# A two-layer decoder on one core: one weight pool for all stages, two loads on another queue, block transposes further apart, operand addresses at one residue

## The chip, the cores and the metric

The kernel runs on one core of a Trainium2 chip. The time is device microseconds of one execution. Of the kernel before, three runs are shown: 2102.8, 2106.49 and 2108.27 us, median 2106.49.

A core has five engines that run side by side, each with its own instruction stream: TensorE (PE) multiplies matrices and also turns (transposes) tiles, VectorE (DVE) and ScalarE (ACT) work on elements, GpSimd (POOL) does a few small things here, and SyncE (SP) only issues loads and stores (DMA). PE reads its operands from SBUF, the core's working memory, and writes to PSUM, a small memory of eight banks that DVE and ACT read. Engines wait for each other through semaphores.

## The reference

256 tokens of width 2048 pass through two layers; all values are float32. Each layer computes, with RMS norms in front:

- attention of its own kind plus attention to 256 memory tokens. Layer a has native sparse attention: a projection `h @ a_w_in`, compressed keys by a small two-layer network, a block-selected and a windowed branch, gated and added. Layer b reads one shared key/value pair (`rms_norm(h) @ w_kv_shared`) with three dilated windows merged by their softmax denominators.
- an output projection (`@ w_out`) added to h,
- a SwiGLU feed-forward with 5632 hidden columns, added to h:

```
h + (silu(y @ w_gate) * (y @ w_up)) @ w_down,   y = rms_norm(h)
```

A last RMS norm gives the output (256, 2048). The feed-forwards hold most of the arithmetic: three matrices of 2048 x 5632 for each layer.

## The kernel before

**How products are made.** Matmuls take float32 operands in a reduced form, so each operand is split into a high part and a rest: `split` (L75) lets ACT write the rounded high part (L77, or L80 with a gain) and DVE the remainder (L78 or L81). `mm3` (L84) then issues three matmuls: high by high (L86), rest of the activations by high weights (L87), high by rest of the weights (L88). A weight chunk is loaded by `load_w` (L93) into a tile `raw` (128 x 1024) on SP's queue, and split into `whi` and `wlo`. A chunk feeds twelve matmuls of 512 columns: four PSUM banks by three.

**The stages.** There are four, each opened by `open_phase` (L56): attention of layer a, feed-forward of layer a ("fa"), attention of layer b, feed-forward of layer b ("fb"). A stage opens its own weight pool (four `raw`, and three `whi`/`wlo` in attention or two in the feed-forward), its own PSUM pools and further tiles; `phase.close()` frees them. The pools of the next stage take the same memory, and the first instruction that uses such a pool waits until the old one is free. In the feed-forward stages seven PSUM banks hold products and one, `aux`, is for turns; in attention `aux` has three or four.

**Feed-forward.** The 11 blocks of 512 hidden columns are worked in three portions, of 4, 4 and 3 blocks (`PORTIONS`). `Group` (L840) is the work of one block (gate and up) or of one half of a portion's down projection (`Lazy`, L1016). Part of it is done by a seven-product scheme in place of eight: `Group.steps` (L876) has seven steps, each with one product of a quarter weight tile of 1536 columns (`q11` and so on, split into `qhi` and `qlo`; nine matmuls), with sums of weight quarters made by DVE (L885, L892, L900, L912). The rest of a block are plain chunks (`plain`, L920). `run_groups` (L936) lays the seven steps of the next group between the plain chunks of the present one; `spacing` (L931) says how many plain chunks stand before each step.

**Turning a block.** When a block's banks are finished, `gate_up` (L974) makes the hidden values as two tiles `hb` (one for each half of the tokens; ACT L982, DVE L983). They have to be turned before the down projection can use them: `Paired.heads` (L297) gives two steps, each with four transposes by PE into an `aux` bank (L305) and then the evacuation by ACT and DVE. For the columns that take part in the seven-product scheme the values first go to a tile `xf`, DVE makes four sums of it (L277 to L280) and both are split (L281). The residual is turned in the same way after the output projections (`residual_block`, L322; transposes L227 or L290).

**Order.** PE's order is the written one. Side steps are put among the matmuls by ticks: a `Side` (L117) counts one tick for every `mm3`, and a step runs when its tick is reached. What `deferred` collects is taken by the next group or product. For the turns of a block the ticks are 5 and 8 (L985), for the residual 3 and 5 (L327). The order on the other engines and on the queues is fixed when the kernel is built, by a planner that plays the program through with a cost for each instruction (`manual_schedule(engines={PE})`, L1304, leaves it all engines but PE).

**Around the change of stage from "fa" to attention b** (L1045 to L1080): the table `cs` and the mask `mask_b` are loaded on SP's queue, the stored memory keys `mb` on GpSimd's; `scaled_tables` (L346) multiplies the table by the token norms before `rope` uses it at the end of the first product.

Of the kernel before, what the change touches and what calls it, by code (L numbers as in the profile page):

```python
# [41 lines left out]
def decoder_trunk(ctx: ExitStack, tc: tile.TileContext, a: dict, out: bass.AP):  # L42
    nc = tc.nc

    const = ctx.enter_context(tc.tile_pool(name="const", bufs=1))
    dram = ctx.enter_context(tc.tile_pool(name="dram", bufs=1, space=bass.MemoryType.DRAM))
    xp = ctx.enter_context(tc.tile_pool(name="xp", bufs=1))
    small = ctx.enter_context(tc.tile_pool(name="small", bufs=6))
    work = ctx.enter_context(tc.tile_pool(name="work", bufs=1))
    work.tile([P, 96], F32, name="padw")  # L50
    phase = ctx.enter_context(ExitStack())
    aux_stack = ExitStack()
    fbufs = [1]
    fpool = wp = wbufs = mm_ps = aux_ps = mm_tags = None

    def open_phase(name, raws, parts, mms, auxs):  # L56
        nonlocal wp, wbufs, mm_ps, mm_tags, aux_ps
        wp = phase.enter_context(tc.tile_pool(name="w" + name, bufs=1))
        wbufs = raws, parts
        mm_ps = phase.enter_context(tc.tile_pool(name="m" + name, bufs=1, space=PSUM))  # L60
        mm_tags = mms
        phase.enter_context(aux_stack)
        aux_ps = aux_stack.enter_context(tc.tile_pool(name="x" + name, bufs=auxs, space=PSUM))
# [29 lines left out]
    def load_w(src, ncols, gain=None, after=None):  # L93
        ck = src.shape[1] // ncols
        raw = wp.tile([P, 1024], F32, tag="raw", name="raw", bufs=wbufs[0])
        rv = raw[:, :ck * ncols]
        if after is None:
            nc.sync.dma_start(rv, src)
        else:
            for q in range(ck):  # L100
                nc.sync.dma_start(rv[:, q * ncols:(q + 1) * ncols], src[:, q * ncols:(q + 1) * ncols])
                after(q)
        rv = rv.rearrange("p (c n) -> p c n", n=ncols)
        hl = []
        for tag in ("whi", "wlo"):
            t = wp.tile([P, 1024], F32R, tag=tag, name=tag, bufs=wbufs[1])
            hl.append(t[:, :ck * ncols].rearrange("p (c n) -> p c n", n=ncols))
        if gain is None:
            split(hl[0], hl[1], rv)
        else:  # L110
            for c in range(ck):
                split(hl[0][:, c, :], hl[1][:, c, :], rv[:, c, :], gain(c))
        return [(hl[0][:, c, :], hl[1][:, c, :]) for c in range(ck)]
# [73 lines left out]
    const.tile([P, 32], F32, name="padc")  # L187
    open_phase("a", 4, 3, ATT, 3)
    ac = phase.enter_context(tc.tile_pool(name="ac", bufs=1))
# [5 lines left out]
    w2 = ac.tile([P, 2, 2, HD], F32, name="w2")  # L195
    ac.tile([P, 8], F32, name="pada")

# [53 lines left out]
    class Paired:  # L251
# [18 lines left out]
        def new_f(self):  # L270
            return fpool.tile([P, NSL, P], F32, tag="xf", name="xf", bufs=fbufs[0])

        def finish(self, q, f):
            n = 4
            if self.sums:
                n = NSL
                nc.vector.tensor_sub(f[:, 4, :], f[:, 0, :], f[:, 3, :])  # L277
                nc.vector.tensor_sub(f[:, 6, :], f[:, 1, :], f[:, 0, :])
                nc.vector.tensor_sub(f[:, 5, :], f[:, 4, :], f[:, 1, :])
                nc.vector.tensor_add(f[:, 7, :], f[:, 2, :], f[:, 5, :])  # L280
            split(self.S[0][:, q, :n, :], self.S[1][:, q, :n, :], f[:, :n, :])  # L281

# [38 lines left out]

    def residual_block(ps, nb, ssq, op):  # L322
        for tt in range(2):
            hb = h[:, tt, nb * 512:(nb + 1) * 512]
            nc.vector.tensor_add(hb, ps[tt], hb)
            square_sum(ssq[:, tt, nb:nb + 1], hb)
        deferred.extend(at([lambda k2=k2: op.turn(nb, k2) for k2 in range(2)], 3, 5))  # L327

# [272 lines left out]
    def compress(kv, toks):  # L601
# [30 lines left out]
        def turn():  # L632
            e = st["e"]
            tr = aux_tile()
            for i in range(2):
                nc.tensor.transpose(tr[:, i * 60:(i + 1) * 60], e[:, i * P:(i + 1) * P], ident[:60, :60])
            z = work.tile([P, 2, 60], F32, tag="cz", name="cz", bufs=1)
            nc.scalar.activation(z.rearrange("p i m -> p (i m)"), tr[:, :120], AF.Copy)
            s = work.tile([P, 2, 30], F32, tag="cs", name="csg", bufs=1)
            zs = z[:, :, 0:30]  # L640
# [172 lines left out]
    def project_out(name, nk, ready, gi):  # L813
        op = Paired(new_x(), KT, lambda k: gains[:, gi, k:k + 1])
        ssq = new_ssq()
        ob = wblocks(name, 4, nk // CK)
        n = nk // CK
        side = take()
        g = [Gemm(ob[i], osx, 512, nk) for i in range(2)]
        side.rate = max(1, 8 / (2 * ready))  # L820
        for i in range(2):
            g[i].run(0, ready, side)
        side.flush()
        for i in range(2):
            side = take()
            g[i].run(ready, n, side)
            side.flush()
            residual_block(g[i].ps, i, ssq, op)
        for nb in range(2, 4):
            ps = gemm(ob[nb], osx, 512, nk)  # L830
            residual_block(ps, nb, ssq, op)
        return op, finish_rstd(ssq, 4)
# [7 lines left out]
    class Group:  # L840

        def __init__(self, op, quarters, rest, done, rest_done=None):
# [84 lines left out]

    def spacing(n):  # L931

        base = {16: (3, 2, 2, 2, 2, 2, 2), 10: (2, 1, 1, 2, 1, 2, 1), 6: (1, 1, 1, 1, 0, 1, 1)}[n]
        return base, n - sum(base)

    def run_groups(groups):  # L936
        for i, g in enumerate(groups):
# [4 lines left out]
            if nxt is not None and nxt.q is not None:  # L942
                base, left = spacing(n)
                for p, s in enumerate(nxt.steps(side)):
# [15 lines left out]
    def ffn(pre, op, f_r, last):  # L960
        gq, gs = a[pre + "_gu_q"], a[pre + "_gu_s"]
        groups = []
        for pi, (b0, b1) in enumerate(PORTIONS):
# [9 lines left out]

            def gate_up(g, j, hop=hop):  # L974
                up = g.bank[3]
# [4 lines left out]
                for tt in range(2):  # L980
# [3 lines left out]
                    hb.append(t)  # L984
                deferred.extend(at(hop().heads(j, hb), 5, 8))  # L985

# [11 lines left out]
            for n2 in range(2):  # L998
# [13 lines left out]

                groups.append(Lazy(hop, [dq[pi, n2, i] for i in range(4)], [ds[n2, c] for c in range(nk - 2 * NPR)], done, rest_done))
        run_groups(groups)

    class Lazy(Group):  # L1016
        def __init__(self, hop, *args):
            super().__init__(None, *args)
            self.hop = hop

# [6 lines left out]
    def open_ffn(name):  # L1027
        nonlocal fh, fq, fpool
        fbufs[0] = 2
        open_phase(name, 4, 2, FFN, 1)  # L1030
        fh = phase.enter_context(tc.tile_pool(name="h" + name, bufs=1))
# [7 lines left out]
    def to_b(ps, nb):  # L1039
        nonlocal xb  # L1040
        if xb is None:
            xb = Plain()
        residual_block(ps, nb, ssq_b, xb)

# [4 lines left out]

    open_phase("b", 4, 3, ATT, 4)  # L1050
    ac = phase.enter_context(tc.tile_pool(name="acb", bufs=1))
    cs = ac.tile([P, 2, 2, HD], F32, name="cs")
    nc.sync.dma_start(cs, a["cs"])
    pc = stack.enter_context(tc.tile_pool(name="pc", bufs=1))
    att = (pc, 4, 6)
    mask_b = pc.tile([P, 2, 3, T], BF16, name="mask_b")
    nc.sync.dma_start(mask_b, a["mask_b"])
    mb = [pc.tile([P, 1024], F32R, name=f"mb{i}") for i in range(4)]
# [259 lines left out]
```

## Time and profile before

| what | value |
|---|---|
| profiled execution | 2106.48 us, span 2104.7 us |
| PE busy | 2033.8 us (97%), 9417 matmuls |
| weight load of PE | 1680.9 us (80%) |
| DVE busy | 1644.3 us (78%) |
| ACT busy | 1190.3 us (57%) |
| loads and stores | 400.74 MB, mean 190 GB/s |
| mean granted TensorE clock | 0.991 |

Time is read so: busy shares say which engine could set the end; the waits say who waited for whom. In lines of the timeline, the first number is the start in us from the begin of the span, the second the duration, then engine, line of the kernel, operation, output and inputs, shapes; in brackets stands how long the engine was idle before it and what ended that. In lines of stretches, after the width come the busy us of PE, weight load, DVE, ACT and GpSimd with their instruction counts, the granted clock, the share of DMA time and GB/s. SPq and POOLq are DMA issues on those queues.

### The profile page before, as it was taken

Reading aid. Unit: us, or ns where it says so; the run is one execution under the profiler, and the core shown is the slowest. Engines: PE = TensorE matmul, PEld = TensorE weight load, DVE = VectorE, ACT = ScalarE, POOL = GpSimd, SP = SyncE. Lnnn points to the kernel's source line nnn. Section 1 sums busy time; section 2 is a strip of 40 time slices with the busy share of each in tenths; the row PEclk is TensorE's granted clock in tenths of the full one; section 3 lists DMA queues with packets and bytes.
Section 4 is the critical chain, followed back from the end, with each engine's and each line's share of the span. In section 5 each row is a group of like instructions: output and inputs, shape, how many; then the busy total and the mean of one; then the engine's idle time right before and its main releaser. Section 6 shows DMA issues by size and latency. Waiting matters only on the chain.

```text
span 2104.7 us, 25507 instructions
## 1 busy us (share of the span) xinstructions
PE 2033.8 (97%) x9417; PEld 1680.9 (80%) x9417; DVE 1644.3 (78%) x2097; ACT 1190.3 (57%) x1552; POOL 9.6 (0%) x30
## 2 busy tenths in 40 slices
PE   9999999999999999999988999989999999999998
PEld 7888888778778887788876788868778887788886
DVE  6677897578888888787876678768888888888755
ACT  7656666556555565555654555656555555555544
POOL 0000000000000000000000000000000000000000
PEclk9999999999999999999999999999999999999999
DMA  8857634476555665556542754366655665556454
GB/s 311 274 184 244 206 102 146 140 251 203 180 180 194 217 199 180 174 203 223 190 169 80 233 171 150 111 252 198 199 175 185 204 216 188 181 186 216 149 193 158
DMA packets 104669, 400.74 MB, mean 190 GB/s; under 512 B 12128, under 2 KB 12512, under 8 KB 104160
## 3 DMA queue, kind: packets, MB, share of 16 engines
q1 hardware_dynamic: 103680, 395.97, 56.5%
q0 software_dynamic: 576, 2.10, 0.3%
q8 instruction: 74, 1.21, 0.2%
q10 hardware_dynamic: 288, 1.05, 0.1%
q14 instruction: 51, 0.42, 0.1%
HBM read 394.87 MB, written 4.19 MB: 190 GB/s over the span
## 4 chain that ended last, share of the span: by engine, by line
PE 84%; DVE 9%; issue 3%; DMA 2%; ACT 2%; SPq 0%; DVEq 0%; POOLq 0%; POOL 0%; ACTq 0%
PE mm L86 26%; PE mm L87 26%; PE mm L88 26%; DVE wlo L78 3%; DVE qlo L78 2%; DVE q L885 1%; PE aux L227 1%; ACT qhi L77 1%; PE aux L305 1%; PE aux L88 1%; PE aux L87 1%; PE aux L86 1%; ACT whi L77 1%; DVE hTlo L78 1%; DVE hb L983 1%
## 5 line engine op out<-in xcount | busy, mean ns | idle before, releaser
L77 ACT ACTIVATE whi<-raw 128x1024 fp32r<-128x1024 f32 (+1 forms) x476 | 498.0, 1047 | 522.0 <-PE mm L87 451.2
L78 DVE TENSOR_TENSOR wlo<-raw,whi 128x1024 fp32r<-128x1024 f32 (+1 forms) x476 | 573.4, 1206 | 214.5 <-ACT whi L77 212.8
L86 PE MATMUL mm<-whi,xhi 128*128 128x512 f32 (+1 forms) x1376 | 540.1, 393 | 19.1 <-ACT whi L77 9.8
L88 PE MATMUL mm<-wlo,xhi 128*128 128x512 f32 (+1 forms) x1376 | 533.8, 388 | 0.8 <-DVE wlo L78 0.7
L87 PE MATMUL mm<-whi,xlo 128*128 128x512 f32 (+1 forms) x1376 | 533.0, 387 | 0.0
L78 DVE TENSOR_TENSOR qlo<-q,qhi 128x1536 fp32r<-128x1536 f32 x210 | 368.5, 1757 | 97.2 <-ACT qhi L77 95.5
L77 ACT ACTIVATE qhi<-q 128x1536 fp32r<-128x1536 f32 x210 | 311.8, 1485 | 135.5 <-PE mm L87 128.2
L86 PEld LDWEIGHTS mm<-whi,xhi 128*128 128x128 f32 x1376 | 260.7, 189 | 68.3 <-ACT whi L77 10.6
L88 PEld LDWEIGHTS mm<-wlo,xhi 128*128 128x128 f32 x1376 | 260.3, 189 | 57.0 <-DVE wlo L78 3.5
L87 PEld LDWEIGHTS mm<-whi,xlo 128*128 128x128 f32 x1376 | 260.8, 190 | 48.2
L86 PE MATMUL mm<-whi,hThi 128*128 128x512 f32 x464 | 181.3, 391 | 0.0
L88 PE MATMUL mm<-wlo,hThi 128*128 128x512 f32 x464 | 180.8, 390 | 0.4 <-DVE wlo L78 0.4
L87 PE MATMUL mm<-whi,hTlo 128*128 128x512 f32 x464 | 180.6, 389 | 0.0
L88 PE MATMUL mm<-qlo,xhi 128*128 128x512 f32 x420 | 163.9, 390 | 1.2 <-DVE qlo L78 1.2
L86 PE MATMUL mm<-qhi,xhi 128*128 128x512 f32 x420 | 164.3, 391 | 0.0
L87 PE MATMUL mm<-qhi,xlo 128*128 128x512 f32 x420 | 163.5, 389 | 0.0
L81 DVE SCALAR_TENSOR_TENSOR wlo<-raw,gains,whi 128x512 fp32r<-128x512 f32 x160 | 113.8, 748 | 50.6 <-ACT whi L80 50.3
L80 ACT ACTIVATE whi<-raw,gains 128x512 fp32r<-128x512 f32 x160 | 107.6, 716 | 64.6 <-PE mm L87 49.4
L86 PE MATMUL mm<-whi,ohi 128*128 128x512 f32 x256 | 101.7, 397 | 1.7 <-ACT whi L80 1.7
L88 PEld LDWEIGHTS mm<-wlo,hThi 128*128 128x128 f32 x464 | 87.1, 188 | 19.0 <-DVE wlo L78 0.8
L87 PEld LDWEIGHTS mm<-whi,hTlo 128*128 128x128 f32 x464 | 87.2, 188 | 17.8
L86 PEld LDWEIGHTS mm<-whi,hThi 128*128 128x128 f32 x464 | 87.1, 188 | 17.7
(273 smaller groups left out, 2471.5 us busy)
## 6 DMA issues: line engine op xcount, KB each, us to landing
raw<-in_a_gu_s_dram SPq DMA_DIRECT2D x100, 512.0 KB, 4.0
raw<-in_b_gu_s_dram SPq DMA_DIRECT2D x100, 512.0 KB, 3.7
q<-in_a_gu_q_dram SPq DMA_DIRECT2D x40, 768.0 KB, 5.5
q<-in_b_gu_q_dram SPq DMA_DIRECT2D x40, 768.0 KB, 5.5
raw<-in_a_dn_s_dram SPq DMA_DIRECT2D x52, 512.0 KB, 3.6
raw<-in_b_dn_s_dram SPq DMA_DIRECT2D x40, 512.0 KB, 3.9
q<-in_a_dn_q_dram SPq DMA_DIRECT2D x24, 768.0 KB, 5.5
raw<-in_a_w_out_dram SPq DMA_DIRECT2D x32, 512.0 KB, 3.5
```

Of the source, the lines that this page charges most:

```text
L77: nc.scalar.activation(hi, src, AF.Copy)
L78: nc.vector.tensor_sub(lo, src, hi.bitcast(F32))
L80: nc.scalar.activation(hi, src, AF.Copy, scale=gain)
L81: nc.vector.scalar_tensor_tensor(lo, src, gain, hi.bitcast(F32), op0=ALU.mult, op1=ALU.subtract)
L86: nc.tensor.matmul(o, l[0], r[0], start=start, stop=False, skip_group_check=more)
L87: nc.tensor.matmul(o, l[1], r[0], start=False, stop=False, skip_group_check=more)
L88: nc.tensor.matmul(o, l[0], r[1], start=False, stop=stop, skip_group_check=more)
L227: nc.tensor.transpose(ps[:, i * P:(i + 1) * P], s, ident)
L305: nc.tensor.transpose(ps[:, i * P:(i + 1) * P], tok[tt][:, i * P:(i + 1) * P], ident)
L885: nc.vector.tensor_add(self.q11, self.q11, self.q12)
L983: nc.vector.scalar_tensor_tensor(t, (g.bank[2], up)[tt], f_r[:, tt:tt + 1], t, op0=ALU.mult, op1=ALU.mult)
```

## The change

- `wp`, the weight pool, is opened once for the whole kernel, in front of the others: four `raw` and three `whi`/`wlo` in every stage. `open_phase` no longer makes one.
- `cs` and `mask_b` of the second layer are issued from GpSimd's queue.
- The turns of a block go from ticks 5 and 8 to 6 and 14; for the second block of a three-block portion to 4 and 10. The turns of the residual get ticks of their own: 4 and 10 after the last output projection block, and (4, 9), (14, 19), (3, 5), (7, 9) after the last down projection of layer a.
- In the last block of a three-block portion, the next group's steps are laid out by another list: five plain chunks before the first step, none before the second, one before each other.
- `finish` splits the four turned slots first and makes the sums in a tile of their own (`xs`), split after that, so one split of eight slots becomes two of four; `xf` is half as large.
- Padding tiles change in size, and `cz` and `csg` move to another pool, so that tiles start at other addresses.

```diff
     const = ctx.enter_context(tc.tile_pool(name="const", bufs=1))
+    wp = ctx.enter_context(tc.tile_pool(name="wp", bufs=4))
...
-    work.tile([P, 96], F32, name="padw")
+    work.tile([P, 20], F32, name="padw")
...
-    def open_phase(name, raws, parts, mms, auxs):
-        nonlocal wp, wbufs, mm_ps, mm_tags, aux_ps
-        wp = phase.enter_context(tc.tile_pool(name="w" + name, bufs=1))
-        wbufs = raws, parts
+    def open_phase(name, mms, auxs):
+        nonlocal mm_ps, mm_tags, aux_ps
...
-        raw = wp.tile([P, 1024], F32, tag="raw", name="raw", bufs=wbufs[0])
+        raw = wp.tile([P, 1024], F32, tag="raw", name="raw")
...
-            t = wp.tile([P, 1024], F32R, tag=tag, name=tag, bufs=wbufs[1])
+            t = wp.tile([P, 1024], F32R, tag=tag, name=tag, bufs=3)
...
-    ac.tile([P, 8], F32, name="pada")
+    ac.tile([P, 16], F32, name="pada")
...
         def finish(self, q, f):
-            n = 4
+            split(self.S[0][:, q, :4, :], self.S[1][:, q, :4, :], f)
             if self.sums:
-                n = NSL
-                nc.vector.tensor_sub(f[:, 4, :], f[:, 0, :], f[:, 3, :])
...
-            split(self.S[0][:, q, :n, :], self.S[1][:, q, :n, :], f[:, :n, :])
+                s = fpool.tile([P, 4, P], F32, tag="xs", name="xs", bufs=1)
+                nc.vector.tensor_sub(s[:, 0, :], f[:, 0, :], f[:, 3, :])
...
+                split(self.S[0][:, q, 4:, :], self.S[1][:, q, 4:, :], s)
...
-    def residual_block(ps, nb, ssq, op):
+    def residual_block(ps, nb, ssq, op, ticks=(3, 5)):
...
-        deferred.extend(at([lambda k2=k2: op.turn(nb, k2) for k2 in range(2)], 3, 5))
+        deferred.extend(at([lambda k2=k2: op.turn(nb, k2) for k2 in range(2)], *ticks))
...
-            residual_block(ps, nb, ssq, op)
+            residual_block(ps, nb, ssq, op, (3, 5) if nb == 2 else (4, 10))
...
-    def spacing(n):
+    def spacing(n, late):
 
         base = {16: (3, 2, 2, 2, 2, 2, 2), 10: (2, 1, 1, 2, 1, 2, 1), 6: (1, 1, 1, 1, 0, 1, 1)}[n]
+        if late:
+            base = (5, 0, 1, 1, 1, 1, 1)
...
-                deferred.extend(at(hop().heads(j, hb), 5, 8))
+                deferred.extend(at(hop().heads(j, hb), *((4, 10) if late and j == 1 else (6, 14))))
...
-                groups.append(Lazy(hop, [dq[pi, n2, i] for i in range(4)], [ds[n2, c] for c in range(nk - 2 * NPR)], done, rest_done))
+                groups.append(Lazy(n2 == 0 and b1 - b0 < 4, hop, [dq[pi, n2, i] for i in range(4)], [ds[n2, c] for c in range(nk - 2 * NPR)], done, rest_done))
...
-        residual_block(ps, nb, ssq_b, xb)
+        residual_block(ps, nb, ssq_b, xb, ((4, 9), (14, 19), (3, 5), (7, 9))[nb])
...
-    nc.sync.dma_start(cs, a["cs"])
+    nc.gpsimd.dma_start(cs, a["cs"])
...
-    nc.sync.dma_start(mask_b, a["mask_b"])
+    nc.gpsimd.dma_start(mask_b, a["mask_b"])
```

More of the change, by code (lines that the diff above doesn't have):

```diff
@@ L53, in decoder_trunk @@
     fbufs = [1]
-    fpool = wp = wbufs = mm_ps = aux_ps = mm_tags = None
-    def open_phase(name, raws, parts, mms, auxs):
-        nonlocal wp, wbufs, mm_ps, mm_tags, aux_ps
-        wp = phase.enter_context(tc.tile_pool(name="w" + name, bufs=1))
-        wbufs = raws, parts
+    fpool = mm_ps = aux_ps = mm_tags = None
+    def open_phase(name, mms, auxs):
+        nonlocal mm_ps, mm_tags, aux_ps
         mm_ps = phase.enter_context(tc.tile_pool(name="m" + name, bufs=1, space=PSUM))
@@ L187, in decoder_trunk @@
     const.tile([P, 32], F32, name="padc")
-    open_phase("a", 4, 3, ATT, 3)
+    open_phase("a", ATT, 3)
     ac = phase.enter_context(tc.tile_pool(name="ac", bufs=1))
@@ L270, in new_f @@
         def new_f(self):
-            return fpool.tile([P, NSL, P], F32, tag="xf", name="xf", bufs=fbufs[0])
+            return fpool.tile([P, 4, P], F32, tag="xf", name="xf", bufs=fbufs[0])
         def finish(self, q, f):
-            n = 4
+            split(self.S[0][:, q, :4, :], self.S[1][:, q, :4, :], f)
             if self.sums:
-                n = NSL
-                nc.vector.tensor_sub(f[:, 4, :], f[:, 0, :], f[:, 3, :])
-                nc.vector.tensor_sub(f[:, 6, :], f[:, 1, :], f[:, 0, :])
-                nc.vector.tensor_sub(f[:, 5, :], f[:, 4, :], f[:, 1, :])
-                nc.vector.tensor_add(f[:, 7, :], f[:, 2, :], f[:, 5, :])
-            split(self.S[0][:, q, :n, :], self.S[1][:, q, :n, :], f[:, :n, :])
+                s = fpool.tile([P, 4, P], F32, tag="xs", name="xs", bufs=1)
+                nc.vector.tensor_sub(s[:, 0, :], f[:, 0, :], f[:, 3, :])
+                nc.vector.tensor_sub(s[:, 2, :], f[:, 1, :], f[:, 0, :])
+                nc.vector.tensor_sub(s[:, 1, :], s[:, 0, :], f[:, 1, :])
+                nc.vector.tensor_add(s[:, 3, :], f[:, 2, :], s[:, 1, :])
+                split(self.S[0][:, q, 4:, :], self.S[1][:, q, 4:, :], s)
         def turn(self, nb, k2):
@@ L636, in turn @@
                 nc.tensor.transpose(tr[:, i * 60:(i + 1) * 60], e[:, i * P:(i + 1) * P], ident[:60, :60])
-            z = work.tile([P, 2, 60], F32, tag="cz", name="cz", bufs=1)
+            z = ac.tile([P, 2, 60], F32, tag="cz", name="cz", bufs=1)
             nc.scalar.activation(z.rearrange("p i m -> p (i m)"), tr[:, :120], AF.Copy)
-            s = work.tile([P, 2, 30], F32, tag="cs", name="csg", bufs=1)
+            s = ac.tile([P, 2, 30], F32, tag="cs", name="csg", bufs=1)
             zs = z[:, :, 0:30]
@@ L840, in decoder_trunk @@
     class Group:
+        late = False
         def __init__(self, op, quarters, rest, done, rest_done=None):
@@ L942, in run_groups @@
             if nxt is not None and nxt.q is not None:
-                base, left = spacing(n)
+                base, left = spacing(n, nxt.late)
                 for p, s in enumerate(nxt.steps(side)):
@@ L972, in hop, with gate_up @@
                 return hp["op"]
-            def gate_up(g, j, hop=hop):
+            def gate_up(g, j, hop=hop, late=b1 - b0 < 4):
                 up = g.bank[3]
@@ L1011, in done, with __init__ @@
                                 nc.vector.tensor_add(hbk, ps[tt], hbk)
-                groups.append(Lazy(hop, [dq[pi, n2, i] for i in range(4)], [ds[n2, c] for c in range(nk - 2 * NPR)], done, rest_done))
+                groups.append(Lazy(n2 == 0 and b1 - b0 < 4, hop, [dq[pi, n2, i] for i in range(4)], [ds[n2, c] for c in range(nk - 2 * NPR)], done, rest_done))
         run_groups(groups)
     class Lazy(Group):
-        def __init__(self, hop, *args):
+        def __init__(self, late, hop, *args):
             super().__init__(None, *args)
-            self.hop = hop
+            self.late, self.hop = late, hop
         def steps(self, side):
@@ L1029, in open_ffn @@
         fbufs[0] = 2
-        open_phase(name, 4, 2, FFN, 1)
+        open_phase(name, FFN, 1)
         fh = phase.enter_context(tc.tile_pool(name="h" + name, bufs=1))
@@ L1048, in decoder_trunk @@
     phase.close()
-    open_phase("b", 4, 3, ATT, 4)
+    open_phase("b", ATT, 4)
     ac = phase.enter_context(tc.tile_pool(name="acb", bufs=1))
     cs = ac.tile([P, 2, 2, HD], F32, name="cs")
-    nc.sync.dma_start(cs, a["cs"])
+    nc.gpsimd.dma_start(cs, a["cs"])
     pc = stack.enter_context(tc.tile_pool(name="pc", bufs=1))
```

## The prediction

> **What bounds the kernel now.** I read the page first, for the busiest engine, then the waits of that engine, then the stretches of granted clock, and last the timeline at each place where the waits sit.
>
> ```profile
> span 2104.7 us, 25507 instructions
> PE 2033.8 (97%) x9417; PEld 1680.9 (80%) x9417; DVE 1644.3 (78%) x2097; ACT 1190.3 (57%) x1552; POOL 9.6 (0%) x30
> ```
>
> PE sets the end. The change takes no matmul away, so it can only win what PE loses: the time it waits, and the time it runs at a lowered clock. The waits of PE (total us, times, longest):
>
> ```profile
> PE aux L305 <- DVE hTlo L78: 23.6, 14, 1.8
> PE mm L86 <- ACT whi L80: 11.0, 3, 9.3
> PE mm L86 <- ACT whi L77: 9.8, 2, 4.9
> PE aux L227 <- DVE xlo L81: 5.4, 2, 2.8
> PE aux L227 <- DVE xlo L78: 2.8, 2, 1.4
> PE mm L86 <- ACT hThi L77: 1.5, 1, 1.5
> PE mm L87 <- DVE hTlo L78: 1.2, 1, 1.2
> ```
>
> L305 are the turns of a finished feed-forward block (four 128x128 transposes each), L227 the turns of the residual, and the long waits of L86 are the three changes of stage. Stretches of the trace, with the granted clock before the last two numbers:
>
> ```profile
> 420.00:434.00 14.00, 10.87 (x32) 8.11 (x33) 8.37 (x9) 5.64 (x8) 0.00 (x0) 0.65 0.78 297
> 526.00:570.00 44.00, 42.48 (x192) 34.91 (x191) 37.06 (x35) 25.59 (x28) 0.00 (x0) 1.00 0.57 186
> 1061.00:1065.00 4.00, 4.00 (x12) 3.13 (x11) 1.76 (x1) 1.97 (x2) 0.00 (x0) 0.57 0.00 0
> 1161.00:1168.00 7.00, 6.54 (x21) 5.34 (x22) 4.25 (x7) 4.54 (x8) 0.00 (x0) 0.56 1.05 394
> 1374.00:1379.00 5.00, 4.09 (x9) 2.79 (x10) 2.45 (x2) 1.88 (x2) 0.00 (x0) 0.52 1.03 404
> ```
>
> After each long wait the clock falls to about half for some microseconds. Width times missing clock gives 14 x 0.35 + 4 x 0.43 + 7 x 0.44 + 5 x 0.48 = 12.1 us; about 1.1 of it fell while PE was still waiting, which leaves 11.0. The ordinary block (526 to 570) keeps its clock in spite of its 1.5 to 1.8 us wait.
>
> **The change part by part.** *One weight pool.* Today each stage has its own pool, and the first load of a stage waits until the old pool is free:
>
> ```profile
> 414.80 0.39 PE L86 MATMUL mm<-whi,ohi 128*128 128x512 f32 x1
> 415.03 0.39 PE L87 MATMUL mm<-whi,olo 128*128 128x512 f32 x1
> 415.25 0.39 PE L88 MATMUL mm<-wlo,ohi 128*128 128x512 f32 x1
> 415.67 1.28 SPq L98 DMA_DIRECT2D raw<-in_a_gu_dram  x3
> 415.68 0.69 DVE L325 TENSOR_TENSOR h<-mm,h 128x512 f32<-128x512 f32 x1 [0.67 <-PE mm L88]
> 420.53 0.79 PE L86 MATMUL mm<-whi,xhi 128*128 128x512 f32 x1 [4.89 <-ACT whi L77]
> ```
>
> The load leaves at 415.67, right after the last matmul of the attention stage (415.25 + 0.39). Landing, rounding and weight loading take the rest of the 4.89 us. With one pool the buffers rotate through the boundary, so up to four raw tiles and two or three rounded ones are ready before the stage ends. What ends last then is the PSUM pool, which still belongs to the stage: the first new matmul has to wait for the residual add at 415.68 (0.69 us), so some 0.8 us of wait stay. The end of the second layer's attention has the same form. The third boundary:
>
> ```profile
> 1150.17 2.73 DVE L325 TENSOR_TENSOR h<-mm,h 128x512 f32<-128x512 f32 x4 [1.31 <-PE mm L88]
> 1152.20 0.33 SPq L1053 DMA_DIRECT2D cs<-in_cs_dram  x1
> 1153.19 23.52 SPq L98 DMA_DIRECT2D raw<-in_w_kv_shared_dram  x10
> 1152.72 1.24 POOL L1060 DMA_DIRECT2D mb<-memkv  x2 [734.36 <-DVE h L325]
> cs<-in_cs_dram SPq DMA_DIRECT2D x1, 256.0 KB, 2.7
> mb<-memkv POOLq DMA_DIRECT2D x4, 512.0 KB, 9.8
> ```
>
> Table and mask stand on SP's queue ahead of the weights, and their tiles lie where the feed-forward tiles were. On one queue they would hold back every prefetch behind them; on GpSimd's they don't. The last add ends at 1152.90, so here too about 0.8 us stay of 9.3. Waits of the three boundaries: 9.3 + 9.8 = 19.1 today, 3 x 0.8 = 2.4 afterwards. The waits that remain are shorter than the 1.8 us of a block turn, after which the clock stays, so the 11.0 us of low clock go too; the piece at 1061 hangs on the next part.
>
> What the move to GpSimd may cost: the scaled tables (four DVE instructions) wait for the cs load, and the weight roundings behind them in DVE's order wait with them. The load may take anything from the 2.7 us of its own row on SP to the 9.8 us of the neighbouring rows on GpSimd's queue. At 2.7 nothing is lost. At 9.8 the tables are done some 12 us after the last matmul, while three rounded chunks of 12 matmuls each (0.227 us apart, by the starts 414.80 to 415.25) and the turns between them keep PE busy for about 11 from its restart: a loss of 2 us or less. I take 0, since the 9.8 us rows ran against ten weight loads, of which four will already be in.
>
> The Trainium skill speaks against this move: "SBUF — State Buffer", box on the "DVE blocks DMA" trap, says that a load from GpSimd's queue needs GpSimd to write its descriptors, and that some DVE instructions lock it out meanwhile. The 9.8 us against 2.7 agree with it. By that rule the sum would be at most the 2 us worse that I keep as a bound.
>
> *Three rounded weight buffers in the feed-forward stages instead of two.* No instruction more; ACT and DVE may run one chunk (12 x 0.227 = 2.7 us) further ahead. DVE is busy 37.06 of 44 us in a block, and 37 of 42 once the wait is gone, so it has the room. I count no gain for it alone.
>
> *Turns further apart.* The feed-forward stages have one PSUM bank for turns, so the second turn waits for the evacuation of the first:
>
> ```profile
> 532.90 0.60 PE L305 MATMUL aux<-ident,hb 128*128 128x128 f32 x4
> 533.82 1.22 DVE L78 TENSOR_TENSOR wlo<-raw,whi 128x1024 fp32r<-128x1024 f32 x1
> 534.96 1.75 DVE L78 TENSOR_TENSOR qlo<-q,qhi 128x1536 fp32r<-128x1536 f32 x1
> 536.63 0.42 DVE L78 TENSOR_TENSOR hTlo<-aux,hThi 128x256 fp32r<-128x256 f32 x1
> ```
>
> The evacuation stands on DVE behind a weight rounding and a quarter rounding and ends at 537.05, 4.15 us after the turn began. The two turns are 3 ticks apart, a tick being three matmuls or 0.68 us: 2.0 us. They go to 6 and 14, 8 ticks or 5.4 us, 1.3 more than the bank needs. So the 23.6 us go. The residual's turns go from two pairs at ticks 3 and 5 to 4, 9, 14, 19 (5 ticks, 3.4 us) and 4, 10 (4.1 us): their evacuation took at most about 3.4, so 5.4 + 2.8 go as well. Splitting pairs costs four more changes between the two kinds of matmul, some 0.1 us each: 0.4.
>
> A later turn can miss its reader. Most blocks are read 30 ticks later. The exception is the last block of the three-block portion, whose tokens the first down product reads directly:
>
> ```profile
> 1103.94 0.68 DVE L78 TENSOR_TENSOR hTlo<-aux,hThi 128x512 fp32r<-128x512 f32 x1
> 1105.38 0.60 ACT L77 ACTIVATE hThi<-aux 128x512 fp32r<-128x512 f32 x1 [2.47 <-PE aux L305]
> ```
>
> Counting plain chunks (4 ticks) and quarter products (3), the reader comes at tick 14 itself, three matmuls after the turn. ACT 0.60 and DVE 0.68 against 0.9 us: at best a wait of 0.6, with a quarter operation (1.75) in front 2.4. I take 1.5.
>
> *Late spacing.* Before the first down product of that portion PE waits 1.5 + 1.2 us for the block before. Moving it from two plain chunks to five puts 10 ticks (6.8 us) between the last turn and its reader: 2.7 gone, and the low clock at 1061 with it. The price is that its second product follows without a chunk between; both roundings can be ready in the five chunks, so 0.
>
> *Two smaller roundings for one.* Per pair sum a rounding of 1024 columns becomes two of 512:
>
> ```profile
> L78 DVE TENSOR_TENSOR hTlo<-xf,hThi 128x1024 fp32r<-128x1024 f32 x15 | 18.1, 1218 | 0.0
> L78 DVE TENSOR_TENSOR hTlo<-aux,hThi 128x512 fp32r<-128x512 f32 x20 | 13.7, 684 | 0.0
> ```
>
> 2 x 684 - 1218 = 150 ns of DVE, and the like on ACT, about 21 times: 3 us spread over DVE's free 15%. On the path 0; without that cover, 3.
>
> *One residue.* By the tiles' sizes, nearly all operands start 224 bytes past a multiple of 256 already; it is the work tiles (hb among them) that move there from 0.
>
> ```profile
> L305 PE MATMUL aux<-ident,hb 128*128 128x128 f32 x176 | 27.1, 276 | 23.6 <-DVE hTlo L78 23.6
> L227 PE MATMUL aux<-ident,E 128*128 128x128 f32 x104 | 15.3, 274 | 1.2 <-DVE E L753 1.2
> ```
>
> Turns of hb (residue 0) and of E (224) take the same, so 0.
>
> **Sum.** Gone: 23.6 + 19.1 + 8.2 + 2.7 + 11.0 = 64.6. Back: 2.4 + 1.5 + 0.4 = 4.3. Net 60.3. The profiled execution took 2106.48 us (span 2104.7), within 0.01 of the median of the runs; 2106.5 - 60.3 gives **2046 us**.
>
> The clock has its own rule in the skill: "TensorE: Matmul & The Clock Gate", "What's actually happening", lowers it after an idle window of about 3.4 us. The row at 1061 fell to 0.57 after waits of 1.5 and 1.2 only, so less suffices here. By either, waits of 0.8 us keep it, and the sum is the same; by the row, a new wait near 3 us would cost 1.7 more.
>
> **Rivals.** (a) The planner that orders ACT and DVE puts evacuations later again because it sees more room, and half of the turn waits and of the residual's stay: (23.6 + 8.2) / 2 = 16, so 2062. For it: the order at 533 to 537, where a turn's evacuation is already last. Against it: 1.3 us of margin and a third buffer. (b) The boundaries don't open: something else of the old stage, the quarter loads or the tables, holds the queue, and half of 19.1 + 9.3 us comes back, 14 or up to 25: 2060 to 2071. For it: SP's queue is in order, and the first quarter load of a stage still waits for old tiles. Against it: that load is first used after three chunks. (c) The change doesn't do what it says, turns and boundaries alike wait on ACT and DVE being late: within 6 us of before. Against it: both engines idle ahead of each wait. (d) Slower: all weights move to the low addresses, and if the new place slows reads, every matmul pays. It decides from 60.3 / 9417 = 6.4 ns per matmul; at 8 ns the result is +15, 2122. For it only that nobody has run this layout; against it the two equal rows of turns.
>
> **How the numbers follow.** Forecast 0.70, its own range 2038 to 2056. (a) 0.12, (b) 0.11, (c) 0.03, (d) 0.04. The range 2038 to 2068 takes in (a) and most of (b), with the bounds 2.4, 2 and 3 above and, below, a boundary wait that vanishes wholly together with single waits under 1 us. About 0.3% (6 us) can be told from no change: faster 0.93, within 0.03, slower 0.04.
>
> **What would show it.** PE's waits of L305 on hTlo fall from 14 to one or two; no wait of L86 on whi over 1.5 us after the start; the clock row is 1.00 at every boundary; weight loads of the next stage leave before the last matmul of the old one; L86 and L88 keep their 0.227 us. The forecast is wrong if PE waits as long in other rows (qlo, wlo or xlo late), or if the step of 0.227 changes.

## The result, and the profile after

The changed kernel takes 2041.69 us (median of four runs, 2040.7 to 2041.91); the kernel before, run beside it, 2107.22 us (2102.8 to 2108.27). The ratio is 0.969, interval 0.9675 to 0.9709. The profiled execution took 2041.91 us. From its page:

```profile
span 2040.1 us, 25602 instructions
PE 2020.5 (99%) x9417; PEld 1676.7 (82%) x9417; DVE 1641.4 (80%) x2118; ACT 1190.4 (58%) x1573; POOL 10.8 (1%) x32
```

The matmuls are the same 9417; PE's busy share went from 97% to 99%. Lines stand one lower than before up to L840: L85 to L87 are now the three matmuls, L76/L77 the split, L304 the turns of a block. All waits of PE after the change that sum to 0.9 us or more (us in total, times, longest):

```profile
PE mm L85 <- ACT whi L79: 1.3, 2, 0.8
PE aux L465 <- DVE warm L462: 1.2, 1, 1.2
PE aux L226 <- DVE E L752: 1.2, 3, 0.4
PE mm L85 <- ACT junk L218: 1.1, 1, 1.1
PE aux L1127 <- DVE E L1119: 1.1, 1, 1.1
PE mm L86 <- DVE hTlo L77: 0.9, 1, 0.9
PE aux L226 <- DVE xlo L80: 0.9, 2, 0.5
PE mm L85 <- ACT whi L76: 0.9, 1, 0.9
PE mm L85 <- DVE h L324: 0.9, 1, 0.9
```

The 14 waits of the block turns are gone and no wait is longer than 1.2 us. The three changes of stage are the rows of L85 on `junk`, on `whi` of L76 and on `h`: 1.1 + 0.9 + 0.9 us. Stretches of the trace over the same places as before (boundary of layer a, an ordinary block, the boundary between the layers, the boundary of layer b); the granted clock is the number before the last two:

```profile
410.00:424.00 14.00, 13.12 (x60) 10.55 (x60) 7.84 (x10) 7.56 (x11) 0.69 (x1) 1.00 0.75 264
518.00:562.00 44.00, 44.00 (x199) 36.41 (x199) 38.50 (x37) 27.43 (x31) 0.00 (x0) 1.00 0.62 200
1119.00:1126.00 7.00, 5.86 (x30) 4.56 (x30) 5.74 (x11) 5.71 (x13) 3.63 (x7) 1.00 0.54 189
1330.00:1336.00 6.00, 6.00 (x30) 4.89 (x28) 3.59 (x6) 4.44 (x7) 0.71 (x1) 1.00 1.02 422
```

The clock is whole at each of them. The timeline at the first boundary, from PE, DVE and SP's queue:

```profile
403.75 13.94 SPq L97 DMA_DIRECT2D raw<-in_a_gu_dram  x6
417.25 1.40 DVE L324 TENSOR_TENSOR h<-mm,h 128x512 f32<-128x512 f32 x2
417.53 0.39 PE L87 MATMUL mm<-wlo,ohi 128*128 128x512 f32 x1
418.79 0.47 PE L85 MATMUL mm<-whi,xhi 128*128 128x512 f32 x1 [0.88 <-ACT whi L76]
```

Loads of the next stage's weights start at 403.75, 14 us ahead of the old stage's last matmul, where they left right behind it before. The next stage starts 0.14 us after the residual add ends (417.25 + 1.40 = 418.65). The row puts its wait down to a rounding that ends at 418.79 itself. At the other two boundaries the start also comes 0.14 and 0.15 us after the end of the add (1121.49 after 1121.35, 1328.76 after 1328.61), so the add most likely ends this wait too.

### The profile page after: what moved, and what is told of

It reads as the page before. It is cut to its first block, busy times and chain, and to the rows that moved or that the text cites. A ratio compares the mean times of both kernels' runs of the same rounds, so it can differ in the third digit from the quotient of the medians.

```text
span 2040.1 us, 25602 instructions
## 1 busy us (share of the span) xinstructions
PE 2020.5 (99%) x9417; PEld 1676.7 (82%) x9417; DVE 1641.4 (80%) x2118; ACT 1190.4 (58%) x1573; POOL 10.8 (1%) x32
## 4 chain that ended last, share of the span: by engine, by line
PE 95%; DVE 2%; ACT 1%; issue 0%; DMA 0%; SPq 0%; DVEq 0%; POOLq 0%; POOL 0%; ACTq 0%
PE mm L85 30%; PE mm L87 30%; PE mm L86 30%; PE aux L304 1%; PE aux L226 1%; DVE wlo L77 1%; PE aux L87 1%; PE aux L86 1%; PE aux L85 1%; PE aux L339 0%; ACT whi L76 0%; PE cmp L625 0%; PE cmp L624 0%; DVE E L377 0%; DMA memT_raw<-in_memT_dram 0%
## 5 line engine op out<-in xcount | busy, mean ns | idle before, releaser
L76 ACT ACTIVATE whi<-raw 128x1024 fp32r<-128x1024 f32 (+1 forms) x476 | 498.4, 1047 | 502.5 <-PE mm L86 461.3
L77 DVE TENSOR_TENSOR wlo<-raw,whi 128x1024 fp32r<-128x1024 f32 (+1 forms) x476 | 573.1, 1205 | 203.9 <-ACT whi L76 202.6
L85 PE MATMUL mm<-whi,xhi 128*128 128x512 f32 (+1 forms) x1376 | 537.5, 391 | 2.9 <-ACT junk L218 1.1
L87 PE MATMUL mm<-wlo,xhi 128*128 128x512 f32 (+1 forms) x1376 | 530.5, 386 | 0.0
L86 PE MATMUL mm<-whi,xlo 128*128 128x512 f32 (+1 forms) x1376 | 529.7, 385 | 0.0
L77 DVE TENSOR_TENSOR qlo<-q,qhi 128x1536 fp32r<-128x1536 f32 x210 | 368.6, 1757 | 75.5 <-ACT qhi L76 74.2
L76 ACT ACTIVATE qhi<-q 128x1536 fp32r<-128x1536 f32 x210 | 311.8, 1486 | 137.8 <-PE mm L86 115.2
L87 PEld LDWEIGHTS mm<-wlo,xhi 128*128 128x128 f32 x1376 | 258.3, 188 | 52.6
L85 PEld LDWEIGHTS mm<-whi,xhi 128*128 128x128 f32 x1376 | 258.6, 188 | 51.0 <-issue 2.5
L86 PEld LDWEIGHTS mm<-whi,xlo 128*128 128x128 f32 x1376 | 258.8, 188 | 47.0
L85 PE MATMUL mm<-whi,hThi 128*128 128x512 f32 x464 | 182.0, 392 | 0.1
L86 PE MATMUL mm<-whi,hTlo 128*128 128x512 f32 x464 | 180.7, 389 | 0.9 <-DVE hTlo L77 0.9
L87 PE MATMUL mm<-wlo,hThi 128*128 128x512 f32 x464 | 180.8, 390 | 0.0
L87 PE MATMUL mm<-qlo,xhi 128*128 128x512 f32 x420 | 163.5, 389 | 0.0
L85 PE MATMUL mm<-qhi,xhi 128*128 128x512 f32 x420 | 163.5, 389 | 0.0
L86 PE MATMUL mm<-qhi,xlo 128*128 128x512 f32 x420 | 163.5, 389 | 0.0
L85 PE MATMUL mm<-whi,ohi 128*128 128x512 f32 x256 | 102.7, 401 | 1.3 <-ACT whi L79 1.3
L86 PEld LDWEIGHTS mm<-whi,hTlo 128*128 128x128 f32 x464 | 87.2, 188 | 19.0 <-DVE hTlo L77 1.2
L85 PEld LDWEIGHTS mm<-whi,hThi 128*128 128x128 f32 x464 | 87.1, 188 | 18.1 <-ACT hThi L76 0.6
L87 PEld LDWEIGHTS mm<-wlo,hThi 128*128 128x128 f32 x464 | 87.1, 188 | 18.1
```

Source lines behind the costliest of these rows:

```text
L76: nc.scalar.activation(hi, src, AF.Copy)
L77: nc.vector.tensor_sub(lo, src, hi.bitcast(F32))
L85: nc.tensor.matmul(o, l[0], r[0], start=start, stop=False, skip_group_check=more)
L86: nc.tensor.matmul(o, l[1], r[0], start=False, stop=False, skip_group_check=more)
L87: nc.tensor.matmul(o, l[0], r[1], start=False, stop=stop, skip_group_check=more)
```

## The experiments

All times are medians beside runs of the kernel before on the same chip (2106.1 to 2106.6 us). A ratio is always to the kernel before.

**The new ticks without the new pool.** The kernel before with the edits on ticks and spacing:

```diff
+            residual_block(ps, nb, ssq, op, (3, 5) if nb == 2 else (4, 10))
...
+        if late:
+            base = (5, 0, 1, 1, 1, 1, 1)
...
+                deferred.extend(at(hop().heads(j, hb), *((4, 10) if late and j == 1 else (6, 14))))
...
+        residual_block(ps, nb, ssq_b, xb, ((4, 9), (14, 19), (3, 5), (7, 9))[nb])
```

> The kernel before with the new ticks of all turns and the late spacing, and nothing else: own weight pools, two rounded buffers, table and mask on SP's queue. My theory (the waits of the turns come from 2.0 us of distance against 4.2 us of evacuation, so distance alone removes them): the 14 waits of L305 (23.6 us), the 8.2 us of L227 and the 2.7 us before the first down product go, with 3 us of low clock behind the latter two: about 38 us less, 2069 us. The three waits at the changes of stage stay at 9.3 and 2 x 4.9. Rival (the evacuation is late because two rounded buffers let ACT and DVE run too little ahead): half of the waits of L305 stay, 2085 us or more.

Measured: 2067.5 us, ratio 0.9811 (0.9795 to 0.9828). Three of its waits, and the stretch behind its first boundary:

```profile
PE mm L86 <- ACT whi L80: 12.1, 3, 10.5
PE mm L86 <- ACT whi L77: 9.6, 2, 4.8
...
PE mm L87 <- DVE hTlo L78: 1.4, 1, 1.4
...
420.00:424.00 4.00, 2.90 (x6) 1.91 (x7) 2.44 (x2) 2.07 (x2) 0.00 (x0) 0.57 1.01 407
```

No block turn waits, with two rounded buffers as before: the ticks alone remove those waits. With the waits of the residual and of the first down product, which are gone too, ticks and spacing win some 39 us of 65. The boundary waits stay, and so does the fall of the clock behind them. The row of L87 on `hTlo` is the last block read at once, with another 0.2 us of L86 on `hThi` ahead of it.

**The new pool without the new ticks.** The changed kernel with ticks and spacing undone (the edit above, reversed).

> The changed kernel with the old ticks (5 and 8, 3 and 5) and the old spacing everywhere; pool, third buffer, queue and addresses as changed. My theory: only the changes of stage are won, 19.1 us of waits less 3 that stay and some 8 of low clock: 24 us less than before, 2083 us, with the 14 waits of L305 back at 1.5 to 1.8 us. Rival (the third rounded buffer lets the evacuation come early): the waits of L305 fall to half or less and the time lies at 2065 us or below.

Measured: 2072.9 us, ratio 0.9837 (0.9823 to 0.9852), ten less than expected. Four of its waits, and the stretches over its first two boundaries:

```profile
PE aux L304 <- DVE hTlo L77: 22.3, 14, 1.8
PE aux L226 <- DVE xlo L80: 3.9, 2, 2.0
PE aux L226 <- DVE xlo L77: 2.8, 2, 1.4
...
PE mm L86 <- DVE hTlo L77: 0.2, 1, 0.2
...
412.00:420.00 8.00, 7.12 (x32) 5.64 (x31) 4.82 (x6) 3.63 (x5) 0.00 (x0) 1.00 0.60 194
...
1119.00:1130.00 11.00, 8.14 (x42) 6.21 (x41) 4.88 (x6) 4.40 (x6) 0.00 (x0) 1.00 0.26 90
```

The turn waits are back, 22.3 + 3.9 + 2.8 us, and the clock stays at 1.00. So the low clock at the boundaries went with the pool, not with the turns. Of the waits ahead of the first down product (L86 on `hTlo` here) 0.2 us is left, though the spacing is the old one; beside the old ticks, the late spacing is not needed for them. The ten us that the expectation missed: it counted 8 us of low clock where all 11.0 went, and it left out 2.5 us ahead of the first down product, 2.8 us of the turns and 2.1 us of L88 on `qlo` and `wlo` (rows further down).

**The tables back on SP's queue.** The changed kernel with one thing undone:

```diff
-    nc.gpsimd.dma_start(cs, a["cs"])
+    nc.sync.dma_start(cs, a["cs"])
...
-    nc.gpsimd.dma_start(mask_b, a["mask_b"])
+    nc.sync.dma_start(mask_b, a["mask_b"])
```

> The changed kernel with table and mask of the second layer loaded on SP's queue again. My theory: they wait there for the feed-forward tiles and hold back every weight load behind them, so the wait at that change of stage returns to 5 to 9 us, with 2 to 3 us of low clock: 7 to 12 us more than the changed kernel, 2049 to 2053 us. Rival (the shared pool alone opens the boundary, the planner having put the weight loads first): within 2 us of 2042.

Measured: 2042.8 us, ratio 0.9696 (0.9682 to 0.9711): the same as the changed kernel. SP's queue at that boundary:

```profile
1103.36 14.34 SPq L97 DMA_DIRECT2D raw<-in_w_kv_shared_dram  x5
1121.32 0.33 SPq L1056 DMA_DIRECT2D cs<-in_cs_dram  x1
```

The planner issues five weight loads ahead of the table, so the table holds nothing back. This boundary opens without the move to GpSimd and, in the next run, without the third buffer; no run has the pool by itself. The move is worth nothing measurable, and costs nothing.

**Two rounded buffers in all stages.** The changed kernel, but

```diff
-            t = wp.tile([P, 1024], F32R, tag=tag, name=tag, bufs=3)
+            t = wp.tile([P, 1024], F32R, tag=tag, name=tag, bufs=2)
```

> The changed kernel with two rounded weight buffers in all stages instead of three (the feed-forward stages had two before, the attention stages three). Theory (the third buffer of the feed-forward stages is worth nothing in itself; the run with the turns alone had two and kept no block-turn wait): 2041 to 2045 us, with small waits on whi or wlo in the attention stages, where a chunk's rounding is now less far ahead. Rival (the buffers carry the new stage across the boundary and keep the evacuations short): waits of L85 and L87 on whi and wlo of 10 us or more in all, 2052 us or more.

Measured: 2088.1 us, ratio 0.9912 (0.9898 to 0.9925). My theory's time was 43 us off. Its longest rows of waits in attention a (the first 455 us), and behind the mark those of the feed-forward of layer a (455 to 1161 us):

```profile
PE mm L87 <- DVE wlo L77: 15.9, 15, 3.1
PE cmp L625 <- DVE wlo L77: 5.8, 7, 1.1
...
PE aux L226 <- DVE xlo L80: 1.8, 1, 1.8
PE mm L86 <- DVE hTlo L77: 1.4, 1, 1.4
PE mm L85 <- ACT whi L76: 0.9, 1, 0.9
```

The loss sits mostly in attention a, which had three buffers before and lost one here: the stage behind it starts at 455.84, where it started at 418.79, 37 of the 46 us. The feed-forwards, which got the third buffer from the change, wait hardly more without it, and the boundaries open all the same. So both theories fell in part: the rival's time and waits came, but not at the boundaries; the buffer that the change adds is worth about nothing, and the third buffer is needed where it was already. The timeline and the stretches at one of the long waits:

```profile
294.25 0.39 PE L86 MATMUL mm<-whi,xlo 128*128 128x512 f32 x1
297.72 0.79 PE L87 MATMUL mm<-wlo,xhi 128*128 128x512 f32 x1 [3.08 <-DVE wlo L77]
...
296.80:303.60 6.80, 5.88 (x17) 4.75 (x18) 3.26 (x5) 0.30 (x1) 0.00 (x0) 0.50 0.45 154
```

The clock is halved for 6.8 us around the end of a single wait of 3.08 us.

**Five ticks between the turns of a block instead of eight.** The changed kernel, but

```diff
-                deferred.extend(at(hop().heads(j, hb), *((4, 10) if late and j == 1 else (6, 14))))
+                deferred.extend(at(hop().heads(j, hb), *((4, 10) if late and j == 1 else (6, 11))))
```

> The changed kernel with the two turns of a gate/up block at ticks 6 and 11 instead of 6 and 14, so five ticks apart instead of eight. A tick is three matmuls at 0.227 us, so five ticks are 3.4 us against the 4.15 us that the evacuation of a turn took in the profile before. Theory (the wait is evacuation less distance): each of the 14 second turns waits 0.7 to 0.8 us again, some 10 us in all, about 2052 us. Rival (with the weights' third buffer and an ACT that is less behind, an evacuation is shorter than five ticks, and three would have to be exceeded only a little): no waits in the group of block turns, 2042 to 2045 us.

Measured: 2039.7 us, ratio 0.9681 (0.9667 to 0.9694): no wait of L304, and the wait of L86 on `hTlo` is gone. The theory fell. One block's turns and the first evacuation:

```profile
522.55 0.60 PE L304 MATMUL aux<-ident,hb 128*128 128x128 f32 x4
525.59 0.42 DVE L77 TENSOR_TENSOR hTlo<-aux,hThi 128x256 fp32r<-128x256 f32 x1
526.43 0.60 PE L304 MATMUL aux<-ident,hb 128*128 128x128 f32 x4
```

From turn to turn it is 3.88 us, as the first turn's own transposes and a slower step behind them add 0.48 us to five ticks of 0.68; I had left that out. The evacuation ends 3.46 us after its turn began, not 4.15 as in the block shown of before. Five ticks leave 0.4 us, eight leave 2.5.

**The last block of the three-block portion earlier.** The changed kernel with ticks 4 and 10 for its turns too (`late and j >= 1`).

> The changed kernel with the turns of the last block of the three-block portion at ticks 4 and 10 instead of 6 and 14, so that the first down product that reads them directly comes later than their evacuation. Theory (the one wait of L86 on hTlo of 0.9 us, 1.5 us of a step by starts, is the price of tick 14): that wait goes, 2040 us, some 1.5 us less than the changed kernel, which lies within the uncertainty of one comparison, so the waits decide. Rival (it moves to the next chunk): the wait stays or turns up on L85 or L87, 2041 to 2043 us.

Measured: 2040.4 us, ratio 0.9688 (0.9675 to 0.9701). The row of L86 on `hTlo` (0.9 us) is gone from its waits and nothing has taken its place there, which is the theory; the times of this kernel, of the one with five ticks and of the changed kernel cannot be told apart, so neither is shown to beat it.

**Other addresses.** Six runs shift tiles by changing pads; no instruction changes. Residue means a tile's start address in SBUF modulo 256 bytes; it follows from the sizes of the tiles in order, and no view of the profile shows it. First, the work tiles and all behind them (feed-forward and attention tiles, quarter tiles) moved by 48 bytes of pad, which puts them 32 bytes further, at residue 0 modulo 256, while `whi`, `wlo`, `xhi` and `xlo` stay at 224:

```diff
-    work.tile([P, 20], F32, name="padw")
+    work.tile([P, 32], F32, name="padw")
```

> The changed kernel with 48 bytes more of padding in the work pool, so that hb, the turned hidden values, the quarters and the attention tiles start at multiples of 256 bytes while weights and turned tokens stay 224 past one. My theory: addresses don't matter, 2042 us within 6, and matmuls still start 0.227 us apart. Rival (operands at different residues slow the reads): more than 6 us slower, with a longer step between matmuls.

Measured: 2069.5 us, ratio 0.9824 (0.981 to 0.9839), 28 us more than the changed kernel. The theory fell. Groups of matmuls by their operands (busy, mean ns, idle), in the changed kernel and then in this one, where the first group has both operands at one residue and the other two do not:

```profile
L86 PE MATMUL mm<-whi,xlo 128*128 128x512 f32 (+1 forms) x1376 | 529.7, 385 | 0.0
L85 PE MATMUL mm<-whi,hThi 128*128 128x512 f32 x464 | 182.0, 392 | 0.1
L85 PE MATMUL mm<-qhi,xhi 128*128 128x512 f32 x420 | 163.5, 389 | 0.0
```

```profile
L86 PE MATMUL mm<-whi,xlo 128*128 128x512 f32 (+1 forms) x1376 | 532.5, 387 | 0.0
L85 PE MATMUL mm<-whi,hThi 128*128 128x512 f32 x464 | 185.0, 399 | 0.1
L85 PE MATMUL mm<-qhi,xhi 128*128 128x512 f32 x420 | 166.5, 396 | 0.0
...
699.72 0.39 PE L85 MATMUL mm<-qhi,xhi 128*128 128x512 f32 x1
...
700.89 0.40 PE L87 MATMUL mm<-qlo,xhi 128*128 128x512 f32 x1
```

The groups with unequal operands take 7 ns more per matmul, the first 2. In the timeline five steps of such a group take 700.89 - 699.72 = 1.17 us, 0.234 each, where the step was 0.227. Then the same pad 80 bytes longer than in the changed kernel (`[P, 40]`; 64 bytes further):

> The changed kernel with its pad ahead of the work tiles 80 bytes longer, so that work, gate/up outputs, quarter sums and attention tiles start 64 bytes further (residue 32 modulo 256), while weights and xhi/xlo stay at 224. Theory (what counts is the offset of the two operands modulo 256 or 128): as slow as the 32-byte shift, about 2069 us, with whi.hThi some 235 ns apart and whi.xhi 227. Rival (only the offset modulo 64 counts): 2041 to 2043 us, as the changed kernel.

and 144 bytes longer (`[P, 56]`; 128 bytes further):

> As the run before it, but shifted by 128 bytes (residue 96 modulo 256). If the offset modulo 256 counts: about 2069 us. If only the offset modulo 128 (or 64) counts: 2041 to 2043 us.

Measured: 2067.9 us (0.9817, 0.9803 to 0.983) and 2065.8 us (0.9809, 0.9796 to 0.9823). Both stay slow, so the offset must agree modulo 256 at least. Next, everything from the weights on moved together by a longer last pad of the constants (`padc`, 32 to 40 words):

> The changed kernel with the constants' last pad 32 bytes longer, so that weights, xhi/xlo, work, feed-forward and attention tiles all start at residue 0 modulo 256 instead of all at 224. Theory (what counts is that the two operands of a matmul start at the same residue, not which): 2040 to 2044 us, with every 512-column step at 227 ns. Rival (224 itself is the good place, and every tile moved off it is slow): 2065 us or more.

Measured: 2042.1 us, ratio 0.9695 (0.9682 to 0.9708): as the changed kernel. What counts is that the operands agree, not where. One of the slowed groups, in this kernel:

```profile
L85 PE MATMUL mm<-whi,hThi 128*128 128x512 f32 x464 | 182.1, 393 | 0.1
```

By the tiles' sizes, the change itself moves only operands of transposes to another residue. That part alone, done to the kernel before:

```diff
-    work.tile([P, 96], F32, name="padw")
+    work.tile([P, 88], F32, name="padw")
...
+    work.tile([P, 8], F32, name="padz")
     ffn("a", fx, f_r, to_b)
```

> The kernel before with one part of the change alone: the work tiles (hb, rope2 and the token tiles) start 32 bytes lower, at residue 224 modulo 256 instead of 0; a pad of 32 bytes behind them leaves every other tile where it was. Theory (the offset counts only for the two operands of a long matmul, and the work tiles are operands of transposes alone): 2104 to 2109 us, as before, with the turns of hb at 276 ns. Rival (the work tiles' residue takes part in the change's gain): at 1000 steps of 6 ns up to 6 us less, 2100 us.

Measured: 2107.0 us, ratio 1.0002 (0.9993 to 1.0011): nothing. And the changed kernel with the identity and `h` at 224 as well (a pad of 24 words ahead of `ident`, one of 8 ahead of `h`, `padc` dropped):

> The changed kernel with the pads of the constants' pool redistributed, so that the identity and h start at residue 224 modulo 256 too (in the changed kernel they start at 128 and 96); nothing else moves. Theory (a matmul whose two operands start at unequal residues is some 6 ns slower, as the run with the work tiles at another residue showed): the transposes and the few matmuls behind each that are now 229 to 240 ns apart come to 227 ns; about 1000 of them at 6 ns are 6 us, so about 2036 us, faster than the changed kernel. Rival (the steps of 229 to 240 ns behind transposes come from the transposes' own shape, not from addresses): 2041 to 2043 us, no difference.

Measured: 2041.2 us, ratio 0.9691 (0.9678 to 0.9704), as the changed kernel; the turns of `hb` take the 272 ns that they take there. The theory fell for transposes: their addresses don't matter here.

## Why the prediction was right

The forecast was 2046, the result 2041.7. By its steps:

- **Block turns, 23.6 us.** Right: gone, and the run with the ticks alone shows that distance does it. The working was too careful: a distance of five ticks would have done, since the 0.48 us of the first turn itself count and the evacuation came at 3.46 us in the block shown of that run.
- **Boundaries, 19.1 us, of which 2.4 stay.** Right: 1.1 + 0.9 + 0.9 = 2.9 us stay, and the new stage starts 0.14 us after the residual add ends, as forecast. The step about the tables failed: I held that cs and mask on SP's queue would hold back every prefetch behind them. The planner places them behind the prefetches. The rival that the tables hold the queue was as wrong as this step.
- **The GpSimd load.** The cost of 0 was right. It landed faster than the bound that I took from its neighbours, as the table of DMA issues (size, median us from issue to landing) shows:

```profile
cs<-in_cs_dram POOLq DMA_DIRECT2D x1, 256.0 KB, 3.2
```

3.2 us, not 9.8. The rule of the Trainium skill weighed there ("SBUF — State Buffer", box on the "DVE blocks DMA" trap) makes such a load late only behind DVE instructions that lock GpSimd out. DVE was busy from 1118.87 to 1123.34, over the issue of the load at 1120.67, and the load was not late; no run here shows the trap at this place.

- **Low clock, 11.0 us.** Right in size. For the 9.3 us at the boundaries the run without the new ticks shows the cause: the boundary waits. The 1.7 us at 1061 went with the waits of the first down product. The reason given, that waits under 1.8 us keep the clock, was too simple, and that it held was in part luck: in the run with the new ticks alone, waits of 0.2 and 1.4 us close together brought it down to 0.50 for 3.4 us (last section).
- **Residual turns, 8.2 us, and the first down product, 2.7 us.** Both gone but for 0.9 us of L226 on `xlo`. The cause given for the second is only half right. With the new ticks and the late spacing alone the rows of this product are gone; but with the old ticks and spacing in the changed kernel all but 0.2 us stays away too. So the late spacing is not needed there, and which of the other edits does it, no run isolates.
- **The last block read at once, 1.5 us back.** Mechanism right: 0.9 us of wait on L86, and it goes when those turns are placed earlier.
- **Third buffer and two smaller roundings, 0.** The buffer: right for the feed-forward stages, by the run with two. The roundings were not tried by themselves.
- **One residue, 0.** The number is right, measured as 1.0002. The reason was not, and the 0 was luck: I read from two equal rows of transposes that addresses don't matter, and they matter by 5 to 7 ns for the long matmuls. The rival "slower", which needed 6.4 ns per matmul, thus named a mechanism that exists; it did not decide because the new pool kept `whi` and `wlo` at the residue of `xhi` and `hThi`.

**The 4 to 5 us that were missed.** The sum was made of waits as the rows give them. Two rows of before that it left out are gone too:

```profile
PE mm L88 <- DVE qlo L78: 1.2, 3, 0.4
PE mm L88 <- DVE wlo L78: 1.1, 4, 0.4
```

With them the waits that vanish come to 57.6 us (the seven rows of the prediction are 55.3), and the rows of after shown above are 6.0 without those on `warm` and `E`, which were there before in the same size: 51.6 us net, where the terms of the forecast make 49.7. With 11.0 for the clock that is 62.6 of the 64.6 us between the two profiled executions. The rest lies in how a wait is counted. It begins at the modelled end of the matmul before, 0.39 us after its start, though the next could have started after 0.227. At the first boundary of before, the starts 415.25 and 420.53 less 0.227 give 5.05 us lost, the row says 4.89. That is 0.16 us at each wait; by the counts in the rows there are 24 fewer, up to 3.8 us. Against it stands the start of the kernel: in the profiled execution of after, the matmuls of the first product ran at half pace (0.43 us apart) up to 12.6 us, where before has full pace (0.23) from 9.5 us. The first matmul of the next product, before and after:

```profile
97.10 0.28 PE L86 MATMUL mm<-whi,xhi 128*128 128x274 f32 x1
98.79 0.28 PE L85 MATMUL mm<-whi,xhi 128*128 128x274 f32 x1
```

That is 1.7 us lost, although the waits of this product are 0.4 us shorter there (1.3 against 1.7), so the slower pace cost 2.1; 62.6 + 3.8 - 2.1 = 64.3 us against 64.6. This closes the sum by working it out from the rows; no run isolates these two terms.

## What to carry to other kernels

A wait at a change of stage that ends on a weight's rounding is first a question of what its buffers are waiting for: one pool across the stages let the loads leave 14 us early, and the boundaries opened with or without the other queue and the third buffer. A wait that repeats for each block is the distance of two steps against an evacuation, to be read as start to start, the step's own matmuls included. Whoever moves pools should look at where the operands of the long matmuls start: here they must agree modulo 256 bytes, or each pays 5 to 7 ns, some 25 us in this kernel, without any wait in the profile.

## What the hardware showed that was not expected

**Operand addresses.** With both operands of a 512-column matmul at one residue modulo 256 (all at 224, or all at 0), steps are 0.227 us; with the two operands (the one loaded into PE and the one streamed past it) 32 bytes apart the step shown above is 0.234, and with 32, 64 or 128 bytes the kernel takes 2066 to 2070 us in place of 2042. The row of one group at 64 bytes:

```profile
L85 PE MATMUL mm<-whi,hThi 128*128 128x512 f32 x464 | 184.4, 397 | 0.1
```

It has 397 ns where the changed kernel has 392. What in the chip does it is open: the weight load of the next matmul runs beside the present one (weight loads are busy for 82% of the span, matmuls for 99%), and which pair of operands collides was not separated; the group with equal operands loses 2 ns as well, so neighbours may be touched.

**The clock.** It is whole or half, and it falls for 3.4 us or a multiple of that: for 6.8 us in the row 296.80:303.60 above. Waits of 1.8 us at every block (22.3 us in all, in the run without the new ticks) leave it whole, while waits of 1.5 and 1.2 us at 1061 in the kernel before did not. What tells them apart is PE's busy time in the 3.4 us before. Two such stretches of the kernel before, the first right ahead of the fall at 1061, the second at a block turn, after which the clock stayed at 1.00:

```profile
1057.93:1061.34 3.41, 1.23 (x4) 0.83 (x5) 2.62 (x2) 1.17 (x2) 0.00 (x0) 1.00 0.35 135
1532.36:1535.77 3.41, 1.62 (x9) 1.25 (x9) 3.41 (x4) 1.66 (x2) 0.00 (x0) 1.00 0.47 159
```

PE is busy for 1.23 of 3.41 us ahead of the fall, and for 1.62 where there is none. In the run with two buffers it is 1.24 of 3.40 ahead of the fall at 296.8. With the traces cut into such stretches, leaving out the start and the end of the kernel, PE is busy for at most 44% ahead of every fall but one, and for at least 47% where the clock stays. The one is in the run with the new ticks alone, 1.77 of 3.41 us ahead of the fall at 1089.6. The ends of matmuls are modelled, so the bound is rough. The Trainium skill ("TensorE: Matmul & The Clock Gate", "What's actually happening") lowers the clock after an idle window of about 3.4 us: the length agrees with these rows, but here PE did not have to be idle for all of it.
